# A diffusion-transformer block on one core: the last difference of a Strassen group formed in PSUM, and h's sums and T4 spread between the quarter products

## The chip, the core and the metric

The kernel runs on one core of one Trainium2 chip. Its engines are named here as the profile names them: PE (TensorE: matmuls, with PEld for its weight loads), DVE (VectorE), ACT (ScalarE), POOL (GpSimd) and SP (SyncE, which here issues the DMAs). The metric is the device time of one execution in microseconds (us). The kernel before takes 1103.48 us, the median of three runs (1101.72 to 1103.72).

## What is computed

One layer of a hybrid block, in float32. An input x of 1024 tokens by 1024 channels is normalised and modulated to h; one input projection feeds three branches and their gates; each branch is projected and gated, and the sum goes through an output projection and a gated residual.

```python
    h, gate = modulate(x, c, lp['norm_g'], lp['w_ada'], lp['b_ada'])
    z = h @ lp['w_in']                    # 1024 x 1024 by 1024 x 8704
    q = na_query(z, lp['q_norm_g'])
    k, v = na_kv(z[..., A_K:A_Z], lp['k_norm_g'])
    ya = neighbourhood_attention(q, k, v, kc, vc, lp['rpb']) * jax.nn.silu(z[..., A_Z:B_B])
    yb = short_conv_branch(z, lp['conv_short_w'])
    yc = conformer_branch(z, lp['conv_conf_w'], lp['conv_conf_b'], lp['ln_conf_g'], lp['ln_conf_b'])
    x = x + gate * merge_branches(z, ya, yb, yc, lp['w_out_a'], lp['w_out_b'], lp['w_out_c'], lp['w_o'])
...
def short_conv_branch(z, w_conv):
    bg, cg, val, gz = z[..., B_B:B_C], z[..., B_C:B_V], z[..., B_V:B_Z], z[..., B_Z:C_GLU]
    return bg * dw_conv(cg * val, w_conv) * jax.nn.silu(gz)

def conformer_branch(z, w_conv, b_conv, ln_g, ln_b):
    a, g = z[..., C_GLU:C_GLU + D_BRANCH], z[..., C_GLU + D_BRANCH:C_Z]
    u = dw_conv(a * jax.nn.sigmoid(g), w_conv) + b_conv
    u = jax.nn.silu(layer_norm(u, ln_g, ln_b))
    return u * jax.nn.silu(z[..., C_Z:GATES])
...
    ga, gb, gc = jnp.split(jax.nn.sigmoid(z[..., GATES:]), N_BRANCH, axis=-1)
    m = ga * (ya @ w_out_a) + gb * (yb @ w_out_b) + gc * (yc @ w_out_c)
    return m @ w_o
```

Every product is made of float32r halves: an operand is split into a high part (a cast) and a low part (the operand less the high part), and high·high, high·low and low·high are added up in PSUM, three matmuls for one.

## The kernel before

**The stages.** First the modulation, h and the context rows; then attention, two heads at a time (up to about 500 us of the span), with the projections of q, k, v and the GLU between; then the rest of the input projection, as Strassen groups (about 500 to 880); then the merges, the output projection and the residual.

**A Strassen group** (`group`, L865 to L918) makes two column tiles of the projection, 256 output channels by 1024 tokens. Both tiles' weight rows are loaded raw (`raw_rows`, four buffers, the DMA at L874) and cut into a11, a12 (first tile) and a21, a22 (second). h's blocks B11, B21, B22, the sums T1, T2, T3 of such blocks and T4 stand in SBUF, split, for all groups. The weight sums are s1 = a21 + a22 (L881), s2 = s1 − a11, s3 = a11 − a21 (all on POOL) and s4 = a12 − s2 (on the engine that the argument `few` names: POOL, and DVE in the eight groups of branch b). s1 to s4 take turns in five SBUF buffers. `wsplit` casts a sum on ACT (L760) and subtracts for the low half (L761). A product is twelve matmuls of 128 x 128 by 128 x 512 (L847 to L849) into one PSUM bank out of six (`ps_g`):

- f = s2·T2; u2 = f + p1 (L896, DVE), with p1 = a11·B11
- c = s1·T1; v = c + u2 (L900, DVE)
- d = s3·T3; c22 = d + v (L853, DVE), then, in the same bank, d += a22·T4; c21 = d + u2 (L853)
- e = s4·B22; c12 = e + v (L853)
- c11 = p1 + a12·B21

In the trace all sums and differences of L764 stand as `s<-...` and all three of L853's as `c<-...`: `c<-gd,v` is c22, `c<-gd,u` c21 and `c<-ge,v` c12. A generator's two `yield`s and `run` interleave the groups, so that PE does f and c of a group, then a22·T4 of the group before it, then d and e. So the product a22·T4 must wait until DVE has read c22 out of that bank. There are 22 groups in a list `plan` (z of b; then for each quarter of b a start group, a gate group and an end group; then z of c and of a, and gates). Between the adds DVE makes the 31-tap convolution of branch c, one tap to an instruction (L821 and L823, 128 x 1024, accumulated in PSUM, four blocks); ACT copies a block out (L827) and SP stores it (L828).

**Quarters.** PE's slack in attention is filled with the products a11·B11 and a12·B21 of the groups (`first_quarters`), 96 of the matmuls behind attention and the others within. p1 and c11 go to DRAM and are loaded again by their group. They need a pair of weight rows split by `load_w` (L92, the low half on POOL). At the same time POOL forms h's sums: `h_sums(j)` gives T1 to T4 for one block row j by four `whole` (L710) and four `less` (L715) and stores them to DRAM. T1 to T3 are loaded and split when the groups begin (L780); T4 is loaded over the two B-halves that it replaces and split at L739 to L743 (cast on ACT, low half on DVE). `h_sums(0)` and `(1)` stand between the heads; `(2)`, `(3)` and T4 stand ahead of the quarters in the program.

**The order** on each engine is decided by a scheduler from the program's order and the dependencies; within an engine instructions then run in that order, and one that waits holds those behind it. SP's queue likewise: a load that waits for its buffer holds the next DMA.

In attention POOL also makes the bias of the scores (L574) that DVE's softmax step (L600) needs, and PE the scores (`sl`, L596) and the products with v (`py`).

Of the kernel before, what the change touches and what calls it, by code (L numbers as in the profile page):

```python
# [8 lines left out]
F32 = mybir.dt.float32  # L9
# [3 lines left out]
ALU = mybir.AluOpType  # L13
AX = mybir.AxisListType
PSUM = bass.MemoryType.PSUM
DRAM = bass.MemoryType.DRAM

P = 128
# [20 lines left out]
BEHIND = 4  # L39
# [8 lines left out]
def tile_hybrid(ctx: ExitStack, tc, x, xT, cx, cond, crow, ng, w_ada, b_ada, wqkv, wz,  # L48
                wout, wo, qg, kg, rpbs, mask, cs, cf, cfb, lng, lnb, out):
    nc = tc.nc  # L50
    pe, act, dve, pool = nc.tensor, nc.scalar, nc.vector, nc.gpsimd
# [73 lines left out]
    td = [[dram.tile([P, 512], F32, name=f"td{i}{j}") for j in range(4)] for i in range(4)]  # L125
    ZA, BG, CG, BV, BZ, CA, CGL, CZ, GT = 0, 4, 8, 12, 16, 20, 24, 28, 32
    B512 = [slice(0, 512), slice(512, 1024)]
# [19 lines left out]
    ahead_of = [n for n in range(len(plan)) if n not in whole_groups]  # L147
# [115 lines left out]
    def hcols(part, k, sl):  # L263

        o = sl.start // 512
        return hlf[o][k][:, part, sl.start - o * 512 : sl.stop - o * 512]
    chd = dram.tile([KT, P, 2 * L], F32, name="chd")

    def tmp(name="tmp"):
        return rp.tile([P, 512], F32, tag="tmp", name=name)  # L270
# [37 lines left out]
    with tc.tile_pool(name="st", bufs=1) as st, tc.tile_pool(name="ps_t", bufs=1, space=PSUM) as pst:  # L308
# [78 lines left out]
        wa = [load_w_ada(0)]  # L387
# [55 lines left out]
        for k in range(KT):  # L443
            raw = tmp("wraw")[:, :384]
# [70 lines left out]
    with tc.tile_pool(name="at", bufs=1, reuse_waits="tile") as at, \  # L515
# [178 lines left out]
        def first_quarters(ns):  # L694

            begun = None
            for n in (*ns, None):
                new = None
                if n is not None:
                    new = n, load_w(wz[lead(n)], KT, pool), quarter_bank()  # L700
                    quarter_part(0, *new)
                if begun:
                    quarter_part(1, *begun)
                begun = new

        def h_sums(j):

            def whole(o, k):
                t = tmp("hsum")
                pool.tensor_tensor(out=t, in0=hlf[o][k][:, 0].bitcast(F32), in1=hlf[o][k][:, 1].bitcast(F32), op=ALU.add)  # L710
                return t

            def less(i, a, b):

                pool.tensor_tensor(out=b, in0=a, in1=b, op=ALU.subtract)  # L715
                nc.sync.dma_start(td[i][j], b)

            t1, b12 = whole(0, j), whole(1, j)
            less(0, b12, t1)
            b22 = whole(1, 4 + j)  # L720
            less(2, b22, b12)
            less(1, b22, t1)
            b21 = whole(0, 4 + j)
            less(3, b21, t1)
# [3 lines left out]
        for hp in range(4):  # L728
# [4 lines left out]
            if hp < 3:  # L733
                for j in ((), (0,), (1,))[hp]:
                    h_sums(j)
                glu(hp + 1)
        for j in (2, 3):
            h_sums(j)
        for j in range(4):  # L739
            hi, lo = hcols(0, j, B512[1]), hcols(1, j, B512[1])  # L740
            nc.sync.dma_start(lo.bitcast(F32), td[3][j])
            act.copy(hi, lo.bitcast(F32))
            dve.tensor_tensor(out=lo, in0=lo.bitcast(F32), in1=hi.bitcast(F32), op=ALU.subtract)  # L743
        first_quarters(ahead_of[:-BEHIND])
    a1ctx.close()


# [8 lines left out]
    def s512(name, tag="s", bufs=5, dt=F32):  # L756
        return sp.tile([P, 512], dt, tag=tag, name=name, bufs=bufs)
# [5 lines left out]
    def sub(eng, dst, a, b):  # L763
        eng.tensor_tensor(out=dst, in0=a, in1=b, op=ALU.subtract)  # L764

    def pair(t):
        return t[:, 0], t[:, 1]
# [6 lines left out]
    T4 = [pair(hlf[1][j]) for j in range(4)]  # L774
# [26 lines left out]
    gctx = ExitStack()  # L801
    wq = ctx.enter_context(tc.tile_pool(name="wq", bufs=1, side="right", reuse_waits="tile"))
    pctx = gctx
    ps_g = gctx.enter_context(tc.tile_pool(name="ps_g", bufs=6, space=PSUM, reuse_waits="tile"))
    ps_c = gctx.enter_context(tc.tile_pool(name="ps_c", bufs=1, space=PSUM, reuse_waits="tile"))

    def bank(name):
        return ps_g.tile([P, 512], F32, tag="g", name=name)
# [27 lines left out]
    def wsplit(src, eng):  # L836
        hi = wq.tile([P, 512], F32R, tag="wh", name="wh", bufs=8)
        lo = wq.tile([P, 512], F32R, tag="wl", name="wl", bufs=8)
        split(hi, lo, src, eng)
        return hi, lo  # L840

    def product(ps, w, blocks, first, last):
        for j in range(4):
            ks = slice(j * P, j * P + P)
            wh, wl = w[0][:, ks], w[1][:, ks]
            bh, bl = blocks[j]
            pe.matmul(ps, wh, bh, start=first and j == 0, stop=False, skip_group_check=True)  # L847
            pe.matmul(ps, wh, bl, start=False, stop=False, skip_group_check=True)  # L848
            pe.matmul(ps, wl, bh, start=False, stop=last and j == 3, skip_group_check=True)  # L849
# [12 lines left out]
            return sp.tile([P, D], F32, tag="wrs", name="wrs")  # L862
        return wq.tile([P, D], F32, tag="wr", name="wr", bufs=3)

    def group(ct0, ct1, use0, use1, few=pool, raw=None, sums=None, wa=None, wf=None, n=None):  # L865

        p1 = s512("p1", "hs", 4)
        if not raw:
            raw = []
            if n is not None:  # L870
                nc.sync.dma_start(p1, p1d[n])
            for ct in (ct0, ct1):
                r = raw_rows()
                nc.sync.dma_start(r, wz[ct])  # L874
                raw += [r[:, :512], r[:, 512:]]
        a11, a12, a21, a22 = raw
        if sums:
            s1, s2 = sums
        else:
            s1, s2 = s512("s1"), s512("s2")  # L880
            pool.tensor_tensor(out=s1, in0=a21, in1=a22, op=ALU.add)  # L881
            sub(pool, s2, s1, a11)
        s3, s4 = (s512(f"s{i}") for i in (3, 4))
        if n is None:
            a = bank("ga")
            product(a, wa or wsplit(a11, pool), B11, True, True)
            act.copy(p1, a)
        else:
            if n in c11d:
                c11 = tmp("c11")  # L890
                nc.sync.dma_start(c11, c11d[n])
                use0(0, c11)
        f = bank("gf")
        product(f, wf or wsplit(s2, pool), T[1], True, True)
        u2 = ev("u2")
        dve.tensor_tensor(out=u2, in0=f, in1=p1, op=ALU.add)  # L896
        c = bank("gc")
        product(c, wsplit(s1, pool), T[0], True, True)
        v = ev("v")
        dve.tensor_tensor(out=v, in0=c, in1=u2, op=ALU.add)  # L900
        yield
        sub(pool, s3, a11, a21)
        d = bank("gd")
        product(d, wsplit(s3, pool), T[2], True, True)
        use1(1, add(d, v, "c22"))
        conv_step(3)
        if n is None:
            product(a, wsplit(a12, pool), B21, False, True)
            use0(0, a)
            conv_step(2)  # L910
        sub(few, s4, a12, s2)
        e = bank("ge")
        product(e, wsplit(s4, dve), B22, True, True)
        use0(1, add(e, v, "c12"))
        yield
        product(d, wsplit(a22, few), T4, False, True)
        use1(0, add(d, u2, "c21"))
        conv_step(3)  # L918

# [121 lines left out]
    def run(*args, **kw):  # L1041

        g = group(*args, **kw)
        next(g)
        if open_:
            next(open_.pop(), None)
        next(g)
        open_.append(g)

    def gate_out(i):  # L1050
        def use(b, t):
            o = tmp("gate") if b == 0 else t
            act.activation(o, t, AF.Tanh, scale=0.5)
            nc.sync.dma_start(gd[i][:, B512[b]], o)
        return use
# [8 lines left out]
    def b_start(n, i):  # L1064
        u = sp.tile([P, 1026], F32, tag="bu", name="bu", bufs=1)
        pool.memset(u[:, 0:1], 0.0)
        pool.memset(u[:, 1025:1026], 0.0)
        held = {}

        def meet(b, t):  # L1070
            if b == 0 and b not in held and n not in c11d:
                c = tmp("c11")
                act.copy(c, t)
                t = c
            if b in held:
                pool.tensor_tensor(out=u[:, 1 + b * 512 : 513 + b * 512], in0=held[b], in1=t, op=ALU.mult)
            held[b] = t

        run(CG + i, BV + i, meet, meet, dve, n=ahead_n(n))
        return u  # L1080

    def ahead_n(n):
        return n if n in p1d else None

    def b_end(n, i, g, u):
        y = sp.tile([P, S], F32, tag="y", name="by", bufs=2)
        act.activation(y, u[:, 0:S], AF.Identity, scale=cs_t[:, i, 0:1])
        for j in (1, 2):
            dve.scalar_tensor_tensor(out=y, in0=u[:, j : j + S], scalar=cs_t[:, i, j : j + 1], in1=y, op0=ALU.mult, op1=ALU.add)

        def last(b, t):
            z = ev("zb")
            nc.sync.dma_start(z, zbd[i][:, B512[b]])
            (pool if b or n in c11d else dve).tensor_tensor(out=z, in0=t, in1=z, op=ALU.mult)
            pool.tensor_tensor(out=z, in0=z, in1=y[:, B512[b]], op=ALU.mult)
            nc.sync.dma_start(ysd[i][:, B512[b]], z)

        run(BG + i, GT + g, last, gate_out(g), dve, n=ahead_n(n))

    for n, (kind, i, j) in enumerate(plan):  # L1100
        kw = {"n": ahead_n(n)}
# [408 lines left out]
```

## Time and profile before

| | us |
|---|---|
| median of three runs | 1103.48 (1101.72 to 1103.72) |
| the profiled execution | 1104.47 |
| its span, first to last instruction | 1102.4 |
| PE busy | 1069.0 (97%) |
| DVE busy | 777.3 (71%) |
| POOL busy | 653.8 (59%) |
| ACT busy | 549.9 (50%) |
| mean granted clock of PE | 0.989 |

The profile is one execution. Times in it count from the first instruction. A row of a timeline gives the start, the length, the engine, the line of the code, what is written and read, and in brackets how long the engine had been idle and what let it go on. A row of groups gives count, total, mean in ns and the idle time ahead of the group. A matmul is pipelined: its length is not the distance to the next. Names such as `gd`, `ge`, `gf`, `gc` are the banks of d, e, f and c; `wr` and `wrs` are raw weight rows, `wh` and `wl` the halves of a split.

### The profile page before, as it was taken

What the parts mean: (1) busy time and instruction counts of PE and PEld (TensorE: products, weight loads), DVE (VectorE), ACT (ScalarE), POOL (GpSimd) and SP (SyncE); (2) the same over time, 40 slices, a digit from 0 to 9 for tenths busy, and PEclk for the clock granted to TensorE, in tenths of its full rate; (3) what the DMA queues carried; (4) which work ended last, traced back from release to release, by engine and by line L of the source; (5) the groups of instructions that cost most, each with busy time, mean ns of one, the idle gap of its engine ahead of it and who ended that gap; (6) DMA issues with size and microseconds to landing.
All of it is one profiled execution on the core that took longest, in us unless ns stands there. A gap on an engine that the chain in (4) does not pass through costs nothing.

```text
span 1102.4 us, 15993 instructions
## 1 busy us (share of the span) xinstructions
PE 1069.0 (97%) x5270; PEld 912.0 (83%) x5270; DVE 777.3 (71%) x1255; ACT 549.9 (50%) x1172; POOL 653.8 (59%) x666
## 2 busy tenths in 40 slices
PE   6899999999999999999999899899999999999998
PEld 5788998998999778888888678788888887888887
DVE  6985576666766755434996898997962559988664
ACT  6764666667566576666332333233345544425630
POOL 3144966437536974333988776887788471623670
PEclk7999999999999999999999999899999999999999
DMA  9627523303212455349645535466444988462362
GB/s 350 221 77 246 181 60 116 113 34 104 95 65 86 133 187 166 127 153 326 218 143 175 173 122 191 162 203 218 162 144 164 321 315 324 137 246 77 96 222 102
DMA packets 92994, 186.24 MB, mean 169 GB/s; under 512 B 11792, under 2 KB 36752, under 8 KB 92816
## 3 DMA queue, kind: packets, MB, share of 16 engines
q1 hardware_dynamic: 88304, 183.13, 49.3%
q10 hardware_dynamic: 4608, 2.10, 0.7%
q8 instruction: 41, 0.67, 0.3%
q14 instruction: 41, 0.34, 0.1%
HBM read 136.96 MB, written 50.79 MB: 170 GB/s over the span
## 4 chain that ended last, share of the span: by engine, by line
PE 71%; DMA 9%; DVE 6%; POOL 6%; issue 4%; ACT 3%; SPq 1%; POOLq 0%; ACTq 0%; DVEq 0%
PE ops L111 4%; PE ops L109 4%; PE ops L110 4%; PE qps L679 3%; PE qps L680 3%; PE qps L678 3%; PE gd L847 3%; PE gd L848 3%; PE gd L849 3%; PE py L635 3%; PE ps L109 3%; PE ps L110 3%; PE ps L111 3%; PE pp L615 2%; DMA wada<-in_w_ada 2%
## 5 line engine op out<-in xcount | busy, mean ns | idle before, releaser
L823 DVE SCALAR_TENSOR_TENSOR cv<-upad,cf_t,cv 128x1024 f32<-128x1024 f32 x120 | 153.5, 1279 | 1.0
L760 ACT CAST wh<-s 128x512 fp32r<-128x512 f32 x111 | 66.5, 616 | 130.2 <-POOL s L764 83.3
L92 POOL TENSOR_TENSOR wl<-wr,wh 128x384 fp32r<-128x384 f32 (+1 forms) x87 | 85.6, 990 | 72.7 <-ACT wh L90 58.6
L761 POOL TENSOR_TENSOR wl<-s,wh 128x512 fp32r<-128x512 f32 x83 | 113.5, 1378 | 7.6 <-ACT wh L760 7.6
L618 DVE TENSOR_TENSOR plo<-pp,phi 128x256 fp32r<-128x256 f32 (+2 forms) x96 | 54.4, 575 | 41.6 <-ACT phi L617 40.7
L90 ACT CAST wh<-wr 128x384 fp32r<-128x384 f32 (+1 forms) x96 | 45.8, 483 | 40.2 <-PE qps L679 23.0
L680 PE MATMUL qps<-ha,wl 128*128 128x512 f32 x160 | 63.4, 396 | 0.0
L679 PE MATMUL qps<-ha,wh 128*128 128x512 f32 x160 | 63.3, 395 | 0.0
L678 PE MATMUL qps<-ha,wh 128*128 128x512 f32 x160 | 63.2, 396 | 0.0
L574 POOL TENSOR_TENSOR bias<-mk,img 64x96 f32<-64x96 bf16 (+1 forms) x96 | 45.6, 481 | 24.9 <-DVE mn L600 16.4
L617 ACT CAST phi<-pp 128x256 fp32r<-128x256 f32 (+2 forms) x96 | 46.5, 495 | 21.2 <-PE pp L615 20.8
L761 POOL TENSOR_TENSOR wl<-wro,wh 128x512 fp32r<-128x512 f32 x12 | 16.8, 1398 | 54.5 <-ACT wh L760 47.9
L600 DVE CUSTOM_DVE_ANT_0 pt<-sl,bias,mn 128x384 f32<-128x384 f32 (+1 forms) x64 | 37.2, 581 | 16.4 <-PE sl L597 15.4
L615 PE MATMUL pp<-ident,pt 128*128 128x128 f32 x304 | 47.0, 272 | 0.9 <-DVE pt L608 0.8
L847 PE MATMUL gd<-hb,wh 128*128 128x512 f32 x96 | 38.7, 403 | 8.2 <-DVE c L853 8.2
L80 POOL TENSOR_SCALAR ssh<-ssh 128x4 f32<-128x4 f32 (+1 forms) x40 | 11.5, 287 | 58.7 <-DVE ssh L255 55.9
L601 ACT ACTIVATE pt<-sc,mn 128x256 f32<-128x256 f32 x64 | 30.6, 478 | 31.4 <-DVE mn L600 27.9
L615 PEld LDWEIGHTS pp<-ident,pt 128*128 128x128 f32 x304 | 37.8, 140 | 9.0 <-issue 1.5
L608 DVE TENSOR_SCALAR pt<-pt,mn 128x640 f32<-128x640 f32 (+1 forms) x64 | 40.2, 669 | 1.0
L81 POOL TENSOR_TENSOR ssh<-ssh,half_neg 128x4 f32<-128x4 f32 (+1 forms) x40 | 39.0, 975 | 3.0
L109 PE MATMUL ps<-wh,hb 128*128 128x384 f32 x112 | 38.8, 347 | 0.6 <-ACT rawc L224 0.5
L849 PE MATMUL gd<-hb,wl 128*128 128x512 f32 x96 | 38.4, 400 | 0.0
(439 smaller groups left out, 3772.0 us busy)
## 6 DMA issues: line engine op xcount, KB each, us to landing
wr<-in_wz SPq DMA_DIRECT2D x34, 512.0 KB, 3.9
gs<-gd SPq DMA_DIRECT2D x24, 512.0 KB, 4.7
wr<-in_wz SPq DMA_DIRECT2D x52, 192.0 KB, 2.5
wada<-in_w_ada SPq DMA_DIRECT2D x16, 512.0 KB, 8.7
wrf<-in_wo SPq DMA_DIRECT2D x16, 512.0 KB, 3.5
cht<-chd SPq DMA_DIRECT2D x24, 256.0 KB, 3.1
wro<-in_wout SPq DMA_DIRECT2D x24, 256.0 KB, 4.6
p1d<-quarter SPq DMA_DIRECT2D x20, 256.0 KB, 2.5
```

What stands on the lines that cost most here:

```text
L92: lo_eng.tensor_tensor(out=lo[:, :n], in0=raw[:, :n], in1=hi[:, :n].bitcast(F32), op=ALU.subtract)
L109: pe.matmul(ps, ah, bh, start=i == 0, stop=False)
L110: pe.matmul(ps, ah, bl, start=False, stop=False)
L111: pe.matmul(ps, al, bh, start=False, stop=i == n - 1)
L615: pe.transpose(out=pp[:, c * P : c * P + P], in_=src, identity=ident)
L678: pe.matmul(ps, wh, bh, start=k == 0, stop=False, skip_group_check=True)
L679: pe.matmul(ps, wh, bl, start=False, stop=False, skip_group_check=True)
L680: pe.matmul(ps, wl, bh, start=False, stop=k % 4 == 3, skip_group_check=True)
L761: eng.tensor_tensor(out=lo, in0=src, in1=hi.bitcast(F32), op=ALU.subtract)
L823: dve.scalar_tensor_tensor(out=acc, in0=src, scalar=cf_t[:, i, j : j + 1], in1=acc, op0=ALU.mult, op1=ALU.add)
L847: pe.matmul(ps, wh, bh, start=first and j == 0, stop=False, skip_group_check=True)
L849: pe.matmul(ps, wl, bh, start=False, stop=last and j == 3, skip_group_check=True)
```

## The change

Three things are changed.

1. In attention, `first_quarters` is called four times, for the groups 0 to 1, 2 to 4, 5 to 7 and the rest of its list. `h_sums(2)` stands after the first call, `h_sums(3)` after the second, the loads and splits of T4 after the third.
2. s4 is formed in PSUM. `ps_g` has five banks instead of six, and the sixth (`ps_h`, "desk") takes s4: ACT copies a12 into it and DVE subtracts s2 in place. The low half of s4's split, on DVE as before, then reads PSUM. So in the 14 groups in which POOL made s4, DVE makes it now, and ACT has one copy more in each group.
3. `few` is gone: the low half of a22, which DVE made in the eight groups of b, is POOL's everywhere.

```diff
-        for j in (2, 3):
-            h_sums(j)
-        for j in range(4):
-            hi, lo = hcols(0, j, B512[1]), hcols(1, j, B512[1])
-            nc.sync.dma_start(lo.bitcast(F32), td[3][j])
-            act.copy(hi, lo.bitcast(F32))
-            dve.tensor_tensor(out=lo, in0=lo.bitcast(F32), in1=hi.bitcast(F32), op=ALU.subtract)
-        first_quarters(ahead_of[:-BEHIND])
+        cuts = (0,2,5,8, len(ahead_of) - BEHIND)
+        for step, (n0, n1) in enumerate(zip(cuts, cuts[1:])):
+            first_quarters(ahead_of[n0:n1])
+            if step < 2:
+                h_sums(step + 2)
+            elif step == 2:
+                for j in range(4):
+                    hi, lo = hcols(0, j, B512[1]), hcols(1, j, B512[1])
+                    nc.sync.dma_start(lo.bitcast(F32), td[3][j])
+                    act.copy(hi, lo.bitcast(F32))
+                    dve.tensor_tensor(out=lo, in0=lo.bitcast(F32), in1=hi.bitcast(F32), op=ALU.subtract)
...
-    ps_g = gctx.enter_context(tc.tile_pool(name="ps_g", bufs=6, space=PSUM, reuse_waits="tile"))
+    ps_g = gctx.enter_context(tc.tile_pool(name="ps_g", bufs=5, space=PSUM, reuse_waits="tile"))
+    ps_h = gctx.enter_context(tc.tile_pool(name="ps_h", bufs=1, space=PSUM, reuse_waits="tile"))
...
+    def desk(name):
+        return ps_h.tile([P, 512], F32, tag="h", name=name)
...
-    def group(ct0, ct1, use0, use1, few=pool, raw=None, sums=None, wa=None, wf=None, n=None):
+    def group(ct0, ct1, use0, use1, raw=None, sums=None, wa=None, wf=None, n=None):
...
-        s3, s4 = (s512(f"s{i}") for i in (3, 4))
+        s3 = s512("s3")
...
-        sub(few, s4, a12, s2)
+        s4 = desk("s4")
+        act.copy(s4, a12)
+        sub(dve, s4, s4, s2)
         e = bank("ge")
         product(e, wsplit(s4, dve), B22, True, True)
...
-        product(d, wsplit(a22, few), T4, False, True)
+        product(d, wsplit(a22, pool), T4, False, True)
...
-        run(CG + i, BV + i, meet, meet, dve, n=ahead_n(n))
+        run(CG + i, BV + i, meet, meet, n=ahead_n(n))
...
-        run(BG + i, GT + g, last, gate_out(g), dve, n=ahead_n(n))
+        run(BG + i, GT + g, last, gate_out(g), n=ahead_n(n))
```

How the instructions stand on two engines, before and after. First DVE in the Strassen groups, late in b's part of the plan, at the c22 (here `c_7787`) whose reader on PE waits longest; `s_7947` is an s4 and `wl` a low half, `cv` a tap. Before:

```order
L900 TENSOR_TENSOR v<-gc,u_7724 128x512
L823 SCALAR_TENSOR_TENSOR cv<-upad,cf_t,cv 128x1024
L761 TENSOR_TENSOR wl<-s_7824,wh 128x512
L764 TENSOR_TENSOR s_7947<-wr,s_7943 128x512
L823 SCALAR_TENSOR_TENSOR cv<-upad,cf_t,cv 128x1024
L853 TENSOR_TENSOR c_7761<-gd,u_7561 128x512
L823 SCALAR_TENSOR_TENSOR cv<-upad,cf_t,cv 128x1024
L853 TENSOR_TENSOR c_7787<-gd,v 128x512
```

After, at the same place, where the c22 is `c_7800` and the s4 `s_8057`:

```order
L907 TENSOR_TENSOR v<-gc,u_7737 128x512
L830 SCALAR_TENSOR_TENSOR cv<-upad,cf_t,cv 128x1024
L764 TENSOR_TENSOR wl<-s_7924,wh 128x512
L830 SCALAR_TENSOR_TENSOR cv<-upad,cf_t,cv 128x1024
L860 TENSOR_TENSOR c_7774<-gd,u_7573 128x512
L767 TENSOR_TENSOR s_8057<-s_8057,s_7959 128x512
L830 SCALAR_TENSOR_TENSOR cv<-upad,cf_t,cv 128x1024
L860 TENSOR_TENSOR c_7800<-gd,v 128x512
```

The s4 still stands ahead of this c22, two places later: c21 (`c_7774`) is now ahead of it, and one tap instead of two lies between it and c22.

Then POOL in the last part of attention, where `ha` and `hb` are h's high and low halves, `hsum` the sums, and `bias` the scores' bias. Before:

```order
L92 TENSOR_TENSOR wl<-wr,wh 128x384 x2
L237 TENSOR_TENSOR vc<-rawc,vc 128x64 x2
L710 TENSOR_TENSOR hsum<-ha_163 128x512
L710 TENSOR_TENSOR hsum<-hb_528 128x512
L710 TENSOR_TENSOR hsum<-hb_698 128x512
L710 TENSOR_TENSOR hsum<-ha_167 128x512
L92 TENSOR_TENSOR wl<-wr,wh 128x256
L715 TENSOR_TENSOR hsum<-hsum 128x512 x3
L92 TENSOR_TENSOR wl<-wr,wh 128x384
L710 TENSOR_TENSOR hsum<-ha_164 128x512
L710 TENSOR_TENSOR hsum<-hb_580 128x512
L710 TENSOR_TENSOR hsum<-hb_712 128x512
```

After:

```order
L237 TENSOR_TENSOR vc<-rawc,vc 128x64 x2
L92 TENSOR_TENSOR wl<-wr,wh 128x256
L92 TENSOR_TENSOR wl<-wr,wh 128x384 x2
L92 TENSOR_TENSOR wl<-wr,wh 128x256
L92 TENSOR_TENSOR wl<-wr,wh 128x384
L574 TENSOR_TENSOR bias_1341<-mk,img 64x3x48 x4
L92 TENSOR_TENSOR wl<-wr,wh 128x384
L574 TENSOR_TENSOR bias_1341<-mk,img 64x2x48 x4
L92 TENSOR_TENSOR wl<-wr,wh 128x256
L92 TENSOR_TENSOR wl<-wr,wh 128x384 x2
L710 TENSOR_TENSOR hsum<-ha_163 128x512
L710 TENSOR_TENSOR hsum<-hb_528 128x512
```

The first sums now come behind eight bias operations and nine low halves of quarter weights; in the order before, those biases stood among the last of the sixteen sums. The second eight sums stand behind the first eight, with low halves between.

## The prediction

> **What bounds the kernel now.** I read the page's head first, then busy time by stretches, then the waits of the engine that bounds, then the rows around each of its waits. The page's first part:
>
> ```profile
> span 1102.4 us, 15993 instructions
> PE 1069.0 (97%) x5270; PEld 912.0 (83%) x5270; DVE 777.3 (71%) x1255; ACT 549.9 (50%) x1172; POOL 653.8 (59%) x666
> ```
>
> PE (TensorE's matmuls) is busy 97% of the span and the change removes no matmul. So the change can only give back time in which PE stands or runs slowly, and it loses whatever makes PE stand anew. The windows tell in which stretches that is (columns: length, then busy time with count for PE, PEld, DVE, ACT, POOL, then PE's granted clock, DMA share, GB/s):
>
> ```profile
> 350.00:400.00 50.00, 48.37 (x247) 39.68 (x247) 32.62 (x53) 32.14 (x75) 43.24 (x41) 1.00 0.44 144
> 450.00:500.00 50.00, 50.00 (x260) 42.36 (x259) 19.87 (x44) 29.93 (x74) 19.65 (x21) 1.00 0.42 139
> 600.00:712.00 112.00, 103.78 (x445) 84.59 (x444) 95.12 (x98) 33.29 (x57) 86.30 (x71) 0.97 0.49 160
> 712.00:840.00 128.00, 128.00 (x564) 105.93 (x563) 102.42 (x109) 47.94 (x83) 106.06 (x81) 1.00 0.53 175
> 370.00:412.00 42.00, 39.26 (x194) 30.87 (x193) 25.38 (x45) 26.91 (x67) 34.90 (x34) 1.00 0.56 187
> ```
>
> From 712 to 840 the Strassen groups run with PE never idle: 564 matmuls in 128.00 us, 0.227 us each. From 600 to 712 the same work has 112.00 − 103.78 = 8.22 us of idle PE and a clock of 0.97; at 0.227 us its 445 matmuls would take 101.0 us, so 11.0 us are lost there. In the attention stage 450 to 500 is full, while 370 to 412 has 2.74 us of idle PE. These two places are where the change works. The waits of PE between 520 and 840 (total, times, longest), and PE's rows at those waits with two of the matmuls after the last (start, length; in brackets idle before and what ended it):
>
> ```profile
> PE gd L847 <- DVE c L853: 8.2, 4, 3.4
> 612.38 0.47 PE L847 MATMUL gd<-hb,wh 128*128 128x512 f32 x1 [1.21 <-DVE c L853]
> 628.74 0.47 PE L847 MATMUL gd<-hb,wh 128*128 128x512 f32 x1 [2.48 <-DVE c L853]
> 657.29 0.47 PE L847 MATMUL gd<-hb,wh 128*128 128x512 f32 x1 [1.10 <-DVE c L853]
> 707.25 0.77 PE L847 MATMUL gd<-hb,wh 128*128 128x512 f32 x1 [3.43 <-DVE c L853]
> 708.66 0.63 PE L847 MATMUL gd<-hb,wh 128*128 128x512 f32 x1
> 709.09 0.63 PE L848 MATMUL gd<-hb,wh 128*128 128x512 f32 x1
> ...
> ```
>
> There is one kind of wait and there are four of it; I call them A, B, C and D. The product a22·T4 goes on accumulating in the bank that holds d, and may start only when DVE has read c22 out of that bank. After D the matmuls start 0.427 us apart, down to the twelfth; at 0.227 us they would take 12 × 0.20 = 2.4 us less. After A, B and C no such stretch follows.
>
> What made c22 late is in DVE's rows ahead of each wait:
>
> ```profile
> 609.02 1.29 DVE L821 TENSOR_SCALAR cv<-upad,cf_t 128x1024 f32<-128x1024 f32 x1 [8.01 <-ACT cvo L827]
> ...
> 625.03 1.77 DVE L764 TENSOR_TENSOR s<-wr,s 128x512 f32<-128x512 f32 x1 [1.49 <-POOL s L764]
> ...
> 627.91 0.68 DVE L853 TENSOR_TENSOR c<-gd,v 128x512 f32<-128x512 f32 x1
> ...
> 652.98 1.77 DVE L764 TENSOR_TENSOR s<-wr,s 128x512 f32<-128x512 f32 x1 [1.36 <-POOL s L764]
> ...
> 701.76 1.76 DVE L764 TENSOR_TENSOR s<-wr,s 128x512 f32<-128x512 f32 x1 [1.19 <-POOL wl L761]
> ...
> 706.42 0.68 DVE L853 TENSOR_TENSOR c<-gd,v 128x512 f32<-128x512 f32 x1
> ```
>
> At B, C and D, DVE stands 1.2 to 1.5 us at s4 of a later group, for POOL, and then takes 1.77 us for it, with c22 queued behind. At B and C it waits for POOL's s2, a true input. At D it waits for POOL's `wl`, which frees the SBUF buffer that s4 is to be written to. At A it stands at the first tap of a convolution block, because ACT's copy-out of the last block waited for a store.
>
> SP's queue shows why that store was late (start, length):
>
> ```profile
> 596.12 7.02 SPq L874 DMA_DIRECT2D wr<-in_wz  x2
> ...
> 603.72 0.38 SPq L828 DMA_DIRECT2D cvd<-cvo  x1
> ```
>
> The store of `cvo` was issued at 603.72, behind two loads of raw rows over which the queue stood 7.02 us.
>
> **The change part by part.** First, s4 in PSUM and no `few`. The rows that price it (count, busy us, mean ns, idle before), of DVE and POOL between 500 and 880:
>
> ```profile
> L764 DVE TENSOR_TENSOR s<-wr,s 128x512 f32<-128x512 f32 x8 | 11.9, 1481 | 7.3 <-POOL s L764 6.1 <-POOL wl L761 1.2
> L761 DVE TENSOR_TENSOR wl<-s,wh 128x512 fp32r<-128x512 f32 x24 | 25.1, 1048 | 3.7 <-ACT wh L760 3.7
> L853 DVE TENSOR_TENSOR c<-gd,v 128x512 f32<-128x512 f32 x22 | 15.0, 680 | 2.1 <-PE gd L849 2.0
> L764 POOL TENSOR_TENSOR s<-wr,s 128x512 f32<-128x512 f32 x13 | 17.4, 1336 | 0.2
> L761 POOL TENSOR_TENSOR wl<-wr,wh 128x512 fp32r<-128x512 f32 x12 | 16.0, 1336 | 3.7 <-ACT wh L760 3.7
> ```
>
> And the nearest to what is new, from the end stage (880 to 1100): a subtraction from PSUM into PSUM, the low half of a split read from PSUM, and an ACT copy from SBUF to PSUM.
>
> ```profile
> L764 DVE TENSOR_TENSOR ops<-ops,mt 128x512 f32<-128x512 f32 x8 | 5.5, 692 | 0.7 <-ACT mt L1186 0.7
> L761 DVE TENSOR_TENSOR mb<-copy,mb 128x512 fp32r<-128x512 f32 x12 | 8.2, 687 | 8.6 <-ACT mb L760 8.5
> L1337 ACT COPY copy<-mt 128x512 f32<-128x512 f32 x8 | 4.5, 594 | 0.0
> ```
>
> In a group of b (eight of them) DVE now spends 1481 + 1048 ns on s4 and its low half, afterwards 692 + 687: 1.15 us less; and its a22 split goes to POOL, which pays 1.34 us for it. In each of the other 14 groups POOL is rid of s4 (1.34 us) and DVE takes it: 692 + 687 − 1048 = 0.33 us more. ACT gets 22 × 0.594 = 13 us more; it is busy 33.29 of 112 us at the gaps, so I cost that at nothing; without that cover it would delay s4 by 0.6 us. Of all these sums only what stands before c22 counts, since PE bounds.
>
> D: the buffer wait goes, as s4 is no longer in those buffers, and the row's 1.76 becomes 0.69: 1.19 + 1.07 = 2.26 of 3.43 us from DVE's rows alone, and the rest if POOL is earlier. The stretch at half pace goes too, once the stop is short: A, B and C, up to 2.48 us, had none. That is another −2.4 us by the rows. The Trainium skill ("TensorE: Matmul & The Clock Gate", Part 1) lets the clock halve after an idle window of about 3.4 us and come back after about as long a busy one. By its figure the stretch would hold 3.4 us, so 1.7 us of loss, an estimate, against the row's 2.4; the trace agrees on where it happens (3.43 us of idle) and shows it longer.
>
> B and C: 1.07 us of each goes with the shorter operation; the rest is POOL's s2. There the change pulls both ways: POOL gains an a22 split in each group of b, and loses s4 in the groups between them. Raw rows are let go by ACT's copy and POOL instead of DVE's slow subtraction, so the next load can start earlier. That leaves C at 0 and B between 0 and 1.4. A: in the order of the changed kernel the store still stands behind such a load, which waits for POOL's low half of a22, so A keeps 0 to 1.2 us. I take 1.3 us left over all four.
>
> A further reason for less is how the long DVE operations arise: 1481 ns with two SBUF inputs against 680 with one in PSUM. The Trainium skill ("SBUF — State Buffer", SBUF: two separate sides) says that a VectorE operation with two SBUF inputs and a GpSimd operation shut each other out of a shared port pair. By that rule the leftover at B and D would be 0 and the sum 1.3 us better, since POOL would be quicker as well; the trace agrees as to DVE, while no row shows POOL with this partner gone.
>
> What is added: c22 of all 22 groups now stands behind an s4 that may wait for POOL; the desk's one bank makes ACT's copy wait for the last s4's low half; and five banks instead of six tie f of a group to u2 of the group before, and c to v. At the tightest place (D's group) u2 was read, and the bank would be wanted, as follows:
>
> ```profile
> 695.75 0.68 DVE L896 TENSOR_TENSOR u<-gf,p 128x512 f32<-128x512 f32 x1
> 698.21 0.39 PE L847 MATMUL gf<-T,wh 128*128 128x512 f32 x1
> ```
>
> That is 698.21 − 696.43 = 1.8 us to spare, more than DVE's 0.33 us of added work. I put all new waits at +0.8 us; the bounds are 0 (every wait met early) and 4.5 (1.5 us lost in three tight groups).
>
> Second, the spread of h's sums and of T4. POOL runs the sixteen sums of `h_sums(2)` and `(3)` in one stretch, of which these are the first and the last; and DVE stands at T4's low halves:
>
> ```profile
> 360.84 1.29 POOL L710 TENSOR_TENSOR hsum<-ha 128x512 f32<-128x512 f32 x1
> 395.91 1.29 POOL L715 TENSOR_TENSOR hsum<-hsum 128x512 f32<-128x512 f32 x1
> 374.27 1.21 DVE L743 TENSOR_TENSOR hb<-hb 128x512 fp32r<-128x512 f32 x1 [3.86 <-ACT hb L742]
> 375.41 0.60 DVE L600 CUSTOM_DVE_ANT_0 pt<-sl,bias,mn 128x384 f32<-128x384 f32 x1
> PE sl L596 <- DVE mn L600: 1.1, 3, 0.6
> ```
>
> At 374.27 DVE had waited 3.86 us for T4, and the softmax's L600 came right behind; the last row is PE's largest wait from 370 to 412, for that L600. With the sums apart, POOL's bias work for those scores comes before the sums and two of the four T4 splits come some fifty DVE rows later, when POOL is half idle (19.65 of 50 us). Two stay at the old place. Of the 2.74 us I take −2.0; the bounds are 0 (the same quarters merely stand elsewhere) and −2.7. The reloads of h's other sums stand behind all these quarters in the program, so a sum formed some quarters later costs nothing there.
>
> The sum: −8.2 + 1.3 − 2.4 + 0.8 − 2.0 = −10.5 us. The profiled execution took 1104.47 us, its span 1102.4; that is 1.0 us above the median of 1103.48. So the profile would read 1094.0, and the median 1093.0.
>
> **The rivals.** First, *POOL stays late*: s2 is an input of s4 wherever s4 lies. DVE's rows give 1.07 us at B and C and 2.26 at D, and the half pace goes, but A stays whole and no more is won: −(1.1 + 1.1 + 2.3) − 2.4 = −6.9, attention −1, new waits +1.5: −6.4, 1097. For it speaks POOL's a22 work in exactly these groups; against it the loads that start earlier.
>
> Second, *nothing is gained*: the loop c22, raw rows, s1, s2, s4, c22 is the period. POOL's wait then moves and the four stops stay in other places; the gain is the half pace alone, 1101 to 1103. Against it: a group takes 60 × 0.227 = 13.6 us of PE, and from 712 to 840 the same loop never stopped PE.
>
> Third, *slower*: DVE now stands at s4 in every group, for POOL. Where DVE makes s4 today, four of eight groups stop, 8.2/8 = 1.0 us each on average. If the other 14 do the same it is +14 us, less 2 for attention and with the half pace unmended: 1104.5 + 14 − 2 − 1 = 1115.5. It decides where s2 ends after DVE comes to s4, by more than c22 can spare. The tightest place between 720 and 780 is
>
> ```profile
> 772.53 1.29 POOL L764 TENSOR_TENSOR s<-s,wr 128x512 f32<-128x512 f32 x1
> 774.21 0.68 DVE L853 TENSOR_TENSOR c<-gd,v 128x512 f32<-128x512 f32 x1
> 777.96 0.39 PE L847 MATMUL gd<-hb,wh 128*128 128x512 f32 x1
> ```
>
> where s2 ends at 773.8, c22 runs from 774.2 to 774.9, and PE wants the bank at 778.0. For it speaks that s2 comes only 0.4 us ahead; against it, that it could come 3.5 us later before PE stood, and that POOL is rid of s4 in just these groups.
>
> **How the numbers follow.** My forecast has a chance of 0.58, POOL stays late 0.23, no gain 0.08, slower 0.11. The forecast's own span, with attention at 0 or −2.7 and new waits from 0 to 4.5, is 1090 to 1098. The range reaches to the first rival's upper side and up to the second: 1089 to 1102. About 0.2%, 2.2 us, is what a measurement of this kernel can tell from no change: faster 0.80, same 0.09, slower 0.11.
>
> **What would show it.** In the changed profile PE's waits for c22 between 520 and 840 should sum to under 2 us; no stretch should have starts 0.427 us apart; s4 on DVE should take about 0.69 us and its low half about 0.69; 370 to 412 should have under 1 us of idle PE. I am wrong if PE waits for u2 or v, if ACT's desk copy waits long for DVE, or if c22 is late after s4 in groups outside b.

## The result and the profile after

The changed kernel takes 1089.21 us, the median of five runs (1086.76 to 1092.94), against 1103.58 us for the kernel before beside it (five runs, 1101.72 to 1104.13): a ratio of 0.9877, 95% interval 0.9853 to 0.9901. That is 14.4 us less by the medians, where 10.5 were forecast; 1089.21 lies inside the range, 0.21 us above its low end. The profiled execution of the changed kernel took 1091.25 us with a span of 1089.5, so 13.2 us less than the profiled execution before; it lies 2.0 us above the median of its own runs, which spread more than those before.

The page's head of the changed kernel:

```profile
span 1089.5 us, 16045 instructions
PE 1064.1 (98%) x5270; PEld 910.6 (84%) x5270; DVE 760.9 (70%) x1261; ACT 564.5 (52%) x1194; POOL 633.8 (58%) x660
```

The same windows as in the prediction, and 500 to 520, first as it was before:

```profile
500.00:520.00 20.00, 20.00 (x90) 16.58 (x89) 9.42 (x14) 13.08 (x24) 4.88 (x11) 1.00 0.98 353
```

After:

```profile
350.00:400.00 50.00, 50.00 (x263) 42.65 (x263) 30.67 (x59) 36.02 (x84) 27.55 (x32) 1.00 0.36 117
370.00:412.00 42.00, 42.00 (x219) 35.66 (x218) 25.08 (x51) 30.21 (x75) 30.50 (x34) 1.00 0.48 161
500.00:520.00 20.00, 18.42 (x81) 14.92 (x80) 10.16 (x15) 13.38 (x25) 5.84 (x5) 1.00 1.01 359
600.00:712.00 112.00, 112.00 (x496) 92.78 (x495) 101.15 (x107) 41.39 (x70) 88.94 (x74) 1.00 0.52 169
712.00:840.00 128.00, 126.26 (x557) 104.24 (x557) 93.41 (x108) 53.61 (x96) 92.14 (x72) 1.00 0.54 177
```

From 600 to 712 PE now does 496 matmuls in 112 us where it did 445: no idle time and the clock at 1.00. That is all of the 11 us that were lost there. 370 to 412 has no idle PE left. Two new losses stand against it, 1.58 us between 500 and 520 and 1.74 us between 712 and 840. They are PE's only waits from 500 to 840:

```profile
PE gd L854 <- DVE c L860: 1.7, 1, 1.7
PE qps L678 <- ACT quarter L685: 1.6, 1, 1.6
```

What the changed operations cost, in groups of DVE, POOL and ACT from 500 to 880, and first the row of POOL's low halves before:

```profile
L761 POOL TENSOR_TENSOR wl<-s,wh 128x512 fp32r<-128x512 f32 x71 | 97.5, 1385 | 6.2 <-ACT wh L760 6.1
```

After:

```profile
L767 DVE TENSOR_TENSOR s<-s,s 128x512 f32<-128x512 f32 x22 | 15.3, 694 | 12.4 <-POOL s L767 10.9 <-ACT s L919 1.5
L764 DVE TENSOR_TENSOR wl<-s,wh 128x512 fp32r<-128x512 f32 x24 | 16.4, 682 | 3.9 <-ACT wh L763 3.9
L764 POOL TENSOR_TENSOR wl<-s,wh 128x512 fp32r<-128x512 f32 x71 | 91.8, 1307 | 16.4 <-ACT wh L763 16.3
L919 ACT COPY s<-wr 128x512 f32<-128x512 f32 x21 | 12.4, 589 | 27.9 <-DVE wl L764 25.6 <-DMA wr<-in_wz 2.4
```

s4 went from 1481 ns to 694 and its low half from 1048 to 682. POOL's 71 low halves, on which nothing was changed, went from a total of 97.5 us to 91.8. DVE still waits for POOL's s2, 10.9 us in all, but no longer where c22 is late by it. ACT's new copy stands 25.6 us in all for DVE's last low half, which frees the desk; the prediction had named a long wait of this copy as a sign of being wrong, but DVE stands only 1.5 us for the copy, and none of PE's waits here comes from that.

The wait for c22 that is left is the first one of the prediction (A) at another block of the convolution. ACT's row ahead of it:

```profile
747.95 0.69 ACT L834 ACTIVATE cvo<-cv,cfb_t 128x512 f32<-128x512 f32 x1 [5.42 <-DMA cvd<-cvo]
```

SP's row of the store that it waits for:

```profile
743.37 0.59 SPq L835 DMA_DIRECT2D cvd<-cvo  x1
```

DVE's rows, the next block's first tap and c22:

```profile
748.67 1.29 DVE L828 TENSOR_SCALAR cv<-upad,cf_t 128x1024 f32<-128x1024 f32 x1 [4.96 <-ACT cvo L834]
...
751.19 0.68 DVE L860 TENSOR_TENSOR c<-gd,v 128x512 f32<-128x512 f32 x1
```

And PE's:

```profile
752.02 0.47 PE L854 MATMUL gd<-hb,wh 128*128 128x512 f32 x1 [1.74 <-DVE c L860]
```

ACT's second copy-out of a block waits 5.42 us for a store; DVE stands 4.96 us at the next block's first tap, and c22 behind it.

The other wait is of a quarter behind attention; ACT's row of the first group's raw rows before:

```profile
516.98 0.62 ACT L760 CAST ah<-wry 128x512 fp32r<-128x512 f32 x1 [0.52 <-DMA wry<-in_wz]
```

ACT's rows after:

```profile
514.35 0.62 ACT L763 CAST ah<-wry 128x512 fp32r<-128x512 f32 x1 [1.66 <-DMA wry<-in_wz]
514.88 0.58 ACT L919 COPY s<-wry 128x512 f32<-128x512 f32 x1
515.40 0.58 ACT L685 COPY quarter<-qps 128x512 f32<-128x512 f32 x1
```

PE's row:

```profile
516.03 0.50 PE L678 MATMUL qps<-ha,wh 128*128 128x512 f32 x1 [1.58 <-ACT quarter L685]
```

ACT stands at the cast of the first group's raw rows, whose load has not landed, and the copy that would free a quarter's bank is queued behind it. Between the two stands the desk's first copy, which is new and delays the quarter's copy by 0.52 us. The rows' cast starts 2.6 us earlier than before, but ACT stands 1.66 us for them where it stood 0.52. In this stretch the DMA engines are full, as they were before (share 1.01 and 0.98). That the earlier end of attention meets loads that cannot come as much earlier is one reading of this; it is not the whole cause, for the run of the groups alone, with attention as before, has 1.2 us of the same wait, and the run of the spread alone, without the desk's copy, has 0.7.

### The profile page after: what moved, and what is told of

It is laid out like the page before. It is cut to its first block, busy times and chain, and to the rows that moved or that the text cites. A ratio compares the mean times of both kernels' runs of the same rounds, so it can differ in the third digit from the quotient of the medians.

```text
span 1089.5 us, 16045 instructions
## 1 busy us (share of the span) xinstructions
PE 1064.1 (98%) x5270; PEld 910.6 (84%) x5270; DVE 760.9 (70%) x1261; ACT 564.5 (52%) x1194; POOL 633.8 (58%) x660
## 4 chain that ended last, share of the span: by engine, by line
PE 74%; DMA 7%; DVE 6%; POOL 6%; issue 3%; ACT 2%; SPq 1%; ACTq 0%; POOLq 0%; DVEq 0%
PE ops L110 4%; PE ops L109 4%; PE ops L111 4%; PE qps L678 3%; PE py L635 3%; PE qps L680 3%; PE qps L679 3%; PE pp L615 3%; PE ps L111 3%; PE ps L109 3%; PE ps L110 2%; DVE cv L830 2%; DMA wada<-in_w_ada 2%; PE gd L854 2%; PE gd L855 2%
## 5 line engine op out<-in xcount | busy, mean ns | idle before, releaser
L764 POOL TENSOR_TENSOR wl<-s,wh 128x512 fp32r<-128x512 f32 x83 | 107.8, 1311 | 17.9 <-ACT wh L763 17.8
L80 POOL TENSOR_SCALAR ssh<-ssh 128x4 f32<-128x4 f32 (+1 forms) x40 | 11.5, 287 | 60.5 <-DVE ssh L255 57.7
L109 PE MATMUL ps<-wh,hb 128*128 128x384 f32 x112 | 38.8, 347 | 0.6 <-ACT rawc L224 0.5
L111 PE MATMUL ps<-wh,hb 128*128 128x384 f32 x112 | 37.8, 342 | 0.3 <-DVE hb L379 0.3
```

The source lines that it names most:

```text
L109: pe.matmul(ps, ah, bh, start=i == 0, stop=False)
L111: pe.matmul(ps, al, bh, start=False, stop=i == n - 1)
L764: eng.tensor_tensor(out=lo, in0=src, in1=hi.bitcast(F32), op=ALU.subtract)
```

## The experiments

The theory: the waits for c22 came from s4 and its low half on DVE, long because both read two SBUF operands, and from POOL's lateness with s2; in PSUM both are short. The spread of h's sums is worth some 3 us by itself. The rivals: the a22 split's move did it; POOL's relief did it wherever s4 lies; one freed buffer did it; five banks cost something.

**The spread alone** (the kernel before with the `cuts` loop in place of the block ahead of the quarters).

> Only the first part of the change: h's sums and T4 spread between the quarters, the groups as before. If the two parts are independent, PE's small stops in attention (370 to 412) go, 3.9 us, and part of that comes back as a wait of the late quarters near 516, 1.6 to 1.7 us; the four waits for c22 stay at about 8.2 us. So 1.5 to 4 us less than before, 1099.5 to 1102. The rival, that the spread also shifts the groups' loads and with them the four waits, would show in the sum of PE's waits for c22: under 5 us or over 11 us.

1099.67 us (seven runs, 1097.79 to 1100.71) against 1102.99: ratio 0.9964, 0.9950 to 0.9979. The window from 370 to 412:

```profile
370.00:412.00 42.00, 42.00 (x219) 35.68 (x218) 24.35 (x48) 30.04 (x74) 31.30 (x36) 1.00 0.49 163
```

PE's waits from 500 to 840:

```profile
PE gd L850 <- DVE c L856: 7.1, 5, 2.7
PE qps L678 <- ACT quarter L685: 0.7, 1, 0.7
```

The stretch from 370 to 412 is full, and the waits for c22 are still there, 7.1 us of them. So the spread gives 3.3 us, and no gain in the groups shows.

**The groups alone** (desk, five banks, s4 on DVE, a22 on POOL; h's sums as before).

> Only the second and third part: s4 on the PSUM desk with five banks, a22's low half on POOL; h's sums and T4 at their old place. If the four waits and the stretch at half pace are all that this part is worth, less one new wait for c22 of 1.9 us at a convolution block's end, and with the 1.4 us that went in the end stage, 9.5 to 11.5 us less than before: 1092 to 1094. The small stops from 370 to 412 should stay (2.7 us of idle PE). The rival, that the groups gain only together with the spread, would give less than 7 us.

1092.60 us (1090.39 to 1094.77) against 1102.99: ratio 0.9895, 0.9870 to 0.9921. In its profile PE's one wait for c22 is 1.0 us, and 370 to 412 has 1.85 us of idle PE; 2.7 were expected to stay. The quarter's wait behind attention is there too, 1.2 us. By the medians 10.4 us here and 3.3 above add up to 13.7, against 14.4 together: the two parts are independent within what these runs can tell.

**a22 on POOL alone**, everything else as before:

```diff
-        product(d, wsplit(a22, few), T4, False, True)
+        product(d, wsplit(a22, pool), T4, False, True)
```

> Only the third part: a22's low half on POOL in b's groups too, s4 on DVE and POOL in SBUF as before. My theory is that the long s4 subtraction ahead of c22 is the cause of the waits, and that POOL's added work makes s2 later in b's groups: the same or slower, 1102 to 1108, with PE's waits for c22 at 6 to 13 us. The rival, that the release of raw rows by POOL and DVE's lighter queue are what mattered, gives 1096 or less.

1107.51 us (1106.68 to 1111.01): ratio 1.0048, 1.0029 to 1.0067, so 4.5 us slower. PE's waits from 500 to 840:

```profile
PE gd L847 <- DVE c L853: 12.9, 8, 3.7
```

DVE's waits for s2 from 520 to 840:

```profile
DVE s L764 <- POOL s L764: 11.5, 4, 6.5
```

DVE waits 11.5 us for s2 where it was 6.1, and PE stops eight times instead of four. POOL's lateness is real, and this part by itself makes it worse.

**The desk with a22 still on DVE** in b's groups:

```diff
+        s4 = desk("s4")
+        act.copy(s4, a12)
+        sub(dve, s4, s4, s2)
...
         product(d, wsplit(a22, few), T4, False, True)
```

> Only the second part: s4 on the PSUM desk with five banks, a22's low half still on DVE in b's groups. By my theory most of the gain is here: 1092 to 1096, PE's waits for c22 under 3 us. By the rival of the run before it needs the a22 move: 1098 or more.

1096.52 us (1093.36 to 1098.28): ratio 0.9934, 0.9912 to 0.9957. This has the expected sign, and is 3.9 us above the run with a22 on POOL as well; the two intervals only just overlap. So the same move that costs 4.5 us with s4 in SBUF seems to gain with s4 in PSUM. The profile does not show why: its execution was the fastest of its four, 1093.36, and that of the run with a22 on POOL the slowest of its four, 1094.77, so the two profiles stand the other way round than the medians. It has one wait for c22 of 2.3 us where the other has 1.0; the low halves of a22 take DVE 1478 and 906 ns there. That stays open.

**Five banks with the sixth idle** (the kernel before with `bufs=5` for `ps_g`).

> The kernel before with five PSUM banks for the groups instead of six, the sixth left idle. My theory, from 1.8 us to spare at the tightest bank, is that this costs under 1 us: 1102 to 1105, no waits of PE for u or v. The rival, that five banks hold up f and c of the next group, gives 1107 or more with PE waits on u2 or v.

1103.97 us (1102.48 to 1105.37) against 1102.12: ratio 1.0018, 1.0005 to 1.0031. Dearer than I thought: 1.9 us by the medians, while its profile shows 0.2 and 0.3 us of waits for u2 and v, which neither the kernel before nor the changed one has. Where the rest is, that profile does not show.

**s4 on DVE in all groups, in SBUF** (six banks, a22 on POOL):

```diff
-        sub(few, s4, a12, s2)
+        sub(dve, s4, a12, s2)
...
-        product(d, wsplit(a22, few), T4, False, True)
+        product(d, wsplit(a22, pool), T4, False, True)
```

> The engines of the changed groups without the desk: DVE makes s4 in all 22 groups and POOL splits a22 in all, but s4 lies in the SBUF buffers as before, with six banks and no copy by ACT. If it is the place in PSUM that helps (short operations, no buffer to wait for), s4 stays at 1.4 us or more and PE's waits for c22 at 6 us or more: 1099 to 1108. The rival, that POOL being rid of s4 is what helps wherever s4 lies, gives 1095 or less.

1108.49 us (1104.88 to 1111.25): ratio 1.0058, 1.0041 to 1.0074. PE's waits from 500 to 840:

```profile
PE gd L847 <- DVE c L853: 14.5, 10, 3.4
```

The groups of DVE from 500 to 880:

```profile
L764 DVE TENSOR_TENSOR s<-wr,s 128x512 f32<-128x512 f32 x21 | 31.9, 1519 | 20.2 <-POOL s L764 14.9 <-POOL wl L761 5.3
L761 DVE TENSOR_TENSOR wl<-s,wh 128x512 fp32r<-128x512 f32 x24 | 25.2, 1051 | 2.6 <-ACT wh L760 2.6
```

The division of work between engines is that of the changed kernel, and it is 6.4 us slower than before. POOL's relief is not what helps: the place in PSUM is worth the distance to the groups-alone run, 1108.5 to 1092.6. This is also the third rival of the prediction, in being: with s4 on DVE everywhere PE stops ten times.

**The desk without ACT's copy**:

```diff
         s4 = desk("s4")
-        act.copy(s4, a12)
-        sub(dve, s4, s4, s2)
+        sub(dve, s4, a12, s2)
```

> The desk without ACT's copy: DVE subtracts a12 - s2, both in SBUF, straight into the PSUM bank; the rest as in the run with the second and third part only. If the length of s4 comes from two SBUF inputs beside POOL, it takes 1.2 to 1.8 us again, its low half 0.69, and the time lies 1 to 4 us above that run: 1093.5 to 1097. If it comes from an output in SBUF, s4 takes 0.7 us and the time is the same, 1091.5 to 1093.5.

1098.66 us (1095.91 to 1099.98): ratio 0.9965, 0.9952 to 0.9978; 6.1 us above the groups-alone run, more than expected. PE's waits for c22:

```profile
PE gd L851 <- DVE c L857: 4.5, 6, 1.6
```

DVE's groups:

```profile
L764 DVE TENSOR_TENSOR s<-wr,s 128x512 f32<-128x512 f32 x21 | 31.2, 1484 | 13.4 <-POOL s L764 13.3
L761 DVE TENSOR_TENSOR wl<-s,wh 128x512 fp32r<-128x512 f32 x24 | 16.3, 681 | 2.6 <-ACT wh L760 2.6
```

With an output in PSUM but both inputs in SBUF, s4 is as long as ever, 1484 ns; its low half, with one input in PSUM, is short. So it is the two SBUF inputs that make the operation long, but only beside a busy POOL. In the kernel before, the low halves of T1 to T3 read two SBUF tiles as well and are short; they all run from 507 to 517, and POOL is busy 4.88 us from 500 to 520:

```profile
L761 DVE TENSOR_TENSOR T<-T 128x512 fp32r<-128x512 f32 x12 | 8.0, 692 | 8.2 <-ACT T L760 7.5 <-POOL wl L92 0.6
```

ACT's copy of 0.59 us is what buys the short s4. It also lets go of raw rows earlier than DVE would, but that is not where the time lies: POOL's additions stand 26.4 us for raw rows in this run (13.5 and 12.9) and 24.3 in the groups-alone run (12.4 and 11.9).

**Its mirror image**, the copy in PSUM and s4 in SBUF:

```diff
-        s4 = desk("s4")
-        act.copy(s4, a12)
-        sub(dve, s4, s4, s2)
+        c12 = desk("c12")
+        act.copy(c12, a12)
+        s4 = s512("s4")
+        sub(dve, s4, c12, s2)
```

> The mirror image of the run without ACT's copy: ACT copies a12 into the PSUM bank, DVE reads it there and writes s4 into one of the five SBUF buffers, so that s4 is short and its low half, from SBUF and SBUF, is long; the rest as in the run with the second and third part only. If the length of both operations ahead of c22 is what counts, s4 takes 0.7 us, the low half 1.0 us or more, PE's waits for c22 are 2 to 6 us and the time lies between that run (1092.6) and the one with neither in PSUM (1108.5), at 1094 to 1100. The rival, that s4's own length is all that counts, gives 1091.5 to 1094; the rival, that the SBUF buffers s4 gave up are what counts, gives 1100 or more, with DVE waiting for POOL's low halves ahead of s4.

1098.42 us (twelve runs, 1096.13 to 1101.64): ratio 0.9967, 0.9952 to 0.9982. PE's waits for c22:

```profile
PE gd L851 <- DVE c L857: 5.0, 3, 4.0
```

DVE's groups:

```profile
L764 DVE TENSOR_TENSOR s<-c,s 128x512 f32<-128x512 f32 x22 | 15.1, 688 | 20.9 <-POOL s L764 13.3 <-POOL wl L761 7.7
L761 DVE TENSOR_TENSOR wl<-s,wh 128x512 fp32r<-128x512 f32 x24 | 25.6, 1065 | 3.0 <-ACT wh L760 3.0
```

The time is where I put it, but the rows speak for two causes: the low half is long again, 1065 ns, and DVE waits 7.7 us for POOL's low halves ahead of s4, which is the wait for an SBUF buffer. PE's clock was 0.97 from 712 to 840, in which its stop of 4.0 us lies. So the desk gives three things: a short s4, a short low half, and no buffer to wait for. Each half of it alone keeps some 6 us of loss; how the loss of this run divides between the long low half and the buffer, no run separates.

**Six SBUF buffers**, the kernel before with `bufs=6` in `s512`.

> The kernel before with six SBUF buffers for the weight sums instead of five. By my reading only the fourth wait (3.43 us) came from a buffer; it and the 2.4 us at half pace after it should go and the other three stay: 1098 to 1101, waits for c22 at 4 to 6 us. The rival, that the loop through POOL gives back what the buffer wins, leaves 1102 or more.

1104.84 us (1101.11 to 1109.31): ratio 1.0020, 1.0001 to 1.0040. A miss, and it tells against my reading of the fourth wait. DVE's rows there:

```profile
697.13 1.77 DVE L764 TENSOR_TENSOR s<-wr,s 128x512 f32<-128x512 f32 x1 [1.01 <-POOL s L764]
...
704.89 0.68 DVE L853 TENSOR_TENSOR c<-gd,v 128x512 f32<-128x512 f32 x1
```

And PE's:

```profile
705.72 0.76 PE L847 MATMUL gd<-hb,wh 128*128 128x512 f32 x1 [3.47 <-DVE c L853]
```

The buffer wait is gone; DVE waits for POOL's s2 in its place, c22 comes as late, and PE stops for 3.47 us instead of 3.43. From s4 to c22 DVE now runs without a pause.

**The convolution's copy-out in its own input** (on the changed kernel; the input is no longer read then):

```diff
-                y = ev("cvo")
+                y = u[:, B512[b]]
```

> The changed kernel, but ACT copies a finished convolution block out into the block's own padded input, which is no longer read, instead of into one of the four buffers it shares with u2, v and the gates. If the wait for c22 that is left, 1.7 us at a block's end, comes from that shared buffer and SP's queue, it goes: 1.5 to 2 us under the changed kernel, 1086.5 to 1088, and DVE stands under 1 us at the first tap of a block. The rival, that POOL's sums hold the next c22 anyway, gives no change, 1088.5 to 1090.

1087.82 us (1086.24 to 1088.28) against 1103.08: ratio 0.9859, 0.9839 to 0.9880. In its profile PE does not wait for c22 at all; DVE still stands at the first taps, 2.2 us over two of them, where I had said under 1. By the medians this is 1.4 us under the changed kernel, and 0.9 us when each is set against the kernel before that ran beside it (15.3 against 14.4). The two intervals overlap. The profile does not settle it either: that of the next run, without this edit, has no wait for c22 from 500 to 840, so the wait that is left comes and goes without it. That this edit is a gain is not shown.

**The first raw rows ahead of T1 to T3** (on the changed kernel, the loads of `early` moved ahead of `load_t`).

> The changed kernel with the first group's raw rows loaded ahead of T1 to T3 instead of behind them. If PE's 1.6 us at 516 come from ACT's cast of those rows, which stands in front of the copy of a quarter and waits for the load, they go: 1086.5 to 1088.5. The rival, that the loads together fill the DMA engines and T1 is then as late, leaves the time within 1 us of the changed kernel or above, with a wait of PE for T in its place.

1090.48 us (1088.37 to 1093.17): ratio 0.9887, 0.9860 to 0.9915. In the profile, of the fastest of the four executions, the quarter's wait is 0.4 us instead of 1.6, and it is PE's only wait from 500 to 840. But the time is not under the changed kernel's, so by itself this is not a gain that can be measured.

**Both.**

> The changed kernel with the edits of the last two runs together. If the two waits are separate, the gains add up: 1085 to 1087. If each only moves PE's wait elsewhere, 1088 or more.

1087.33 us (1086.19 to 1088.05): ratio 0.9857, 0.9832 to 0.9881. Its profile has no wait of PE from 500 to 840. It beats the kernel before by 15.8 us, and the changed kernel by 1.9 us by the medians (1.4 against the kernel before beside each), again with overlapping intervals.

## Why the prediction was right, and where its sizes were off

The mechanism was the one forecast: the long operations of DVE ahead of c22 became short, the four waits and the half pace went, and attention filled up. That the time fell inside the range is in part luck. The forecast's own span was 1090 to 1098, and by its own terms the sum goes down to −12.0 (1091.5) at most, or −13.3 (1090.2) if nothing is left over of the waits; no term reaches 1089, and two of the five executions lie below it.

**The four waits** (−8.2, of which 1.3 was to stay): right in kind, and nothing stayed at these four places. The leftover at B and D rested on POOL's added a22 work in b's groups. The run with only that shows the added work does hurt as long as DVE's long operations are there; with them gone, POOL is quicker as well (97.5 to 91.8 us for the same 71 low halves). This is what the sentence on the shared port pair had said, and its sum, 1.3 us better, was the nearer one, though the 1.3 also held A's share, which that sentence does not touch. The same 71 low halves of POOL took 103.7 us with both of DVE's operations long in all groups, 100.4 with s4 long, 95.8 with the low half long, and 92.5 and 91.8 with both short. The Trainium skill ("SBUF — State Buffer", SBUF: two separate sides) is borne out by the run without ACT's copy: two SBUF inputs give 1484 ns beside a busy POOL, whatever the output, and 692 ns where POOL is mostly idle.

**Wait D by its own step** failed: I counted 1.19 us for the buffer and 1.07 for s4's length. Taking the buffer wait alone away gave nothing (1104.84). Where s4 was short but still in SBUF, the wait for a buffer came back, 7.7 us of DVE's time; what it cost PE there is not separated from the long low half.

**The half pace** (−2.4): it went, as forecast; no stop longer than 1.74 us is left. The reason I gave, that a short stop has none, is too simple; see the last section.

**New waits** (+0.8): 3.3 us came, neither of them among the kinds I listed. One is A at another block of the convolution, for which I had left 0 to 1.2 us among the leftovers; counted there, the leftover is 1.7 for 1.3, and 1.6 new for 0.8. The other is the quarter's wait behind attention, of which 0.52 us is the desk's own copy by ACT, which I had costed at nothing. Five banks I had put at under 1 us; the run with an idle bank says 1.9 by the medians, 0.5 to 3.4 by the interval times 1102.

**Attention** (−2.0): the idle time from 370 to 412 went whole, 2.74 us, and the spread alone gives 3.3 in the time. The idle time was too small a measure: a matmul's row is longer than the distance to the next (0.39 us against 0.227 in the groups), so short delays do not show as idle. The rest is not idle time outside the window, for from 412 to 500 PE was full before (88.00 of 88.00 us). The distances between the starts of PE's matmuls tell more (us, one profiled execution each, the same number of matmuls in each stretch):

| stretch of PE | before | spread alone | groups alone | changed |
|---|---|---|---|---|
| first instruction to first matmul of `sl` | 115.0 | 113.0 | 114.4 | 114.0 |
| from there to the first matmul of `gf` | 409.0 | 405.5 | 410.2 | 407.6 |
| from there to the groups' last matmul | 357.1 | 356.7 | 346.5 | 347.2 |
| from there to the last matmul | 217.2 | 217.2 | 217.6 | 215.8 |

The spread takes 3.5 us out of the second stretch, of which the changed kernel keeps 1.4: there the quarter's wait of 1.6 stands against it.

**The rest.** The terms as measured, −8.2 − 2.4 − 2.7 + 3.3, make −10.0 of the 13.2 us between the two profiled executions. By the table the changed kernel gains 9.9 us in the groups, 1.4 in attention, 1.4 behind the groups and 1.0 ahead of the scores. The last two I cannot put to the change. The first stretch is 112.7 us in the run with a22 on POOL alone and 113.8 in that with six buffers, neither of which has an edit there; the last is 217.2 and 217.6 us in the runs with one part alone, and 215.7 in the run with six buffers, slower in all. So the terms came to nearly what was forecast, −10.0 for −10.5, because their errors cancel: 1.3 us less left over and 0.7 more from attention stand against 2.5 more of new waits. Most of what the measured gain has beyond them lies where the change has no part, or none that I can show.

**The rivals.** That POOL stays late is true of the kernel with a22 on POOL alone; in the changed one DVE still waits for s2, 10.9 us in all, but PE does not stop for it. The slower one, DVE standing at s4 everywhere, is what the kernel without the desk does, at 1108.5. It needed long operations to come about.

## What to carry to other kernels

A queue that runs in order passes on the length of what stands ahead of the instruction that others wait for: shortening that by a microsecond is worth more than the engine's idle share says. Where VectorE and GpSimd work side by side on SBUF operands, a copy by an idle ScalarE that puts one of VectorE's two operands in PSUM can pay, on both engines: here 1481 ns became 694, and POOL's 71 low halves took 91.8 us instead of 97.5. Try such a change as a whole: here a22's move alone gave +4.5 us, with s4's move between engines +6.4, either half of the desk with both −3.5 to −4.4, and the whole −10.4.

## What the runs showed of the hardware

The half pace after a stop of PE does not need 3.4 us. In the run with the spread alone it followed 2.46 us (start, length, idle before):

```profile
623.88 0.77 PE L850 MATMUL gd<-hb,wh 128*128 128x512 f32 x1 [2.46 <-DVE c L856]
624.45 0.63 PE L851 MATMUL gd<-hb,wh 128*128 128x512 f32 x1
624.87 0.63 PE L852 MATMUL gd<-hb,wl 128*128 128x512 f32 x1
```

In the kernel before, a stop of 2.48 us (B) had none, and one of 3.43 us had twelve slow matmuls; after 2.46 us there were seven. PE's granted clock was 0.97 from 600 to 712 in both profiles. So neither whether it comes nor how long it lasts follows from the stop's length alone. The Trainium skill ("TensorE: Matmul & The Clock Gate", Part 1) speaks of an idle window of about 3.4 us; these rows have it after less.
